# Products of ones in TensorE's idle stretches, and a last MLP product in two halves of the tokens, in an encoder layer on eight cores

## The chip, the cores and the metric

One Trainium2 chip, all eight cores, each with two of the sixteen sequences. The metric is device time in microseconds (us) of the slowest core. Some executions fell into a second, slower state: over 2300 us, with a lower granted TensorE clock on the cores of one die.

## The reference

One layer on x (16 x 2048 x 1024, float32): a grouped-query attention branch and a pooling branch with gates, a cross attention into 256 memory tokens, then the MLP and a final norm. The change touches only the end:

```python
def rmsnorm(x, g):
    xf = x.astype(jnp.float32)
    y = xf * lax.rsqrt(jnp.mean(xf * xf, axis=-1, keepdims=True) + EPS)
    return (y * g.astype(jnp.float32)).astype(x.dtype)
# ... attention, pooling, gates, cross attention ...
        n3 = rmsnorm(h, g_ffn[l])
        h = h + jnp.square(jax.nn.relu(n3 @ w_ff1[l])) @ w_ff2[l]
    return rmsnorm(h, g_final)
```

## The kernel before

The kernel is written as a graph of operations. A scheduler in the program, with its own model of durations, gives each engine a fixed order before anything runs; semaphores keep the order right on the chip. The tokens go through in eight blocks of 512 (two sequences of four). While one block is in its projections and MLP, the attention of the next fills TensorE's gaps; the last block has no next one. The end of a block:

```python
def ff2_step(j):                       # output rows j*128 .. j*128+127, 512 tokens
    def f():
        w = [weight("FB", j), weight("FB", 8 + j)]
        h, H, r = c_["h"][j], c_["H"], c_["r"]
        b = V("f2", "D")               # a PSUM bank
        PE([mm(lambda: ap(b), wsl(w[k // 16], k % 16 * 128), lambda k=k: ap(H[k]), k == 0, k == 31,
               [wk(w[k // 16], k % 16 * 128), H[k]]) for k in range(32)], [b])
        t = V("f2r", "M1")
        D(lambda e: e.tensor_tensor(out=ap(t), in0=ap(b), in1=ap(r), op=ALU.mult), 512, [b, r], [t])
        TT(lambda e: e.tensor_tensor(out=ap(h), in0=ap(t), in1=ap(h), op=ALU.add), [t, h], [h])
        if j >= 1:
            stat_after(j - 1, "s4")    # square on ScalarE, sum over rows by a product with ones
        if j == 7:
            stat_after(7, "s4")
            final()
    return f

def final():
    r = rstd(c_["s4"], 1024.0)         # Ln, then Exp, on ScalarE
    for kc in range(8):
        h = c_["h"][kc]
        D(lambda e, h=h, kc=kc: e.scalar_tensor_tensor(out=ap(h), in0=ap(h), scalar=vec[:, ...], in1=ap(r), ...), 512, ...)
        store(outT[s, tb, kc], lambda h=h: ap(h), 262144, [h], ...)
# ...
order, span, busy = schedule(G, pools, 100000.0, 40000.0)
# ...
emit(nc, st, order)
```

The softmax here doesn't subtract the row's maximum and nothing guards it: scores larger than these inputs give would overflow.

Of the kernel before, what the change touches and what calls it, by code (L numbers as in the profile page):

```python
# [13 lines left out]
EPS = 1e-6  # L14
# [59 lines left out]
NORM1 = (1, 4)  # L74
LAST_NORM = 1
SUMMED = ()
LATE = {("KV", i): 1 for i in range(3)}
LATE.update({("G", i): 1 + i % 2 for i in range(8)})
LATE.update({(name, i): i % 3 for i in range(16) for name in ("FA", "FB")})
# [326 lines left out]



def emit(nc, stack, order):
    engines = ("pe", "act", "dve", "pool", "sp")  # L410
    SEM_CAP = 20000
    allops = sorted((o for e in engines for o in order[e]), key=lambda o: o.place)
    dcount = {}
    plan = {}
    known = {e: {} for e in engines}
    clock = {}
    needed = set()

    def waits_for(e, deps):
        out = []  # L420
        kn = known[e]
        ds = sorted(deps, key=lambda d: -d.finish)
        for d in ds:
            if d.dma is not None:
                s, v = d.key
                if kn.get(("d", s), 0) >= v:
                    continue
                out.append(("d", s, v))
                kn[("d", s)] = v
            else:  # L430
                if d.eng == e and e == "pe":
                    continue
                if kn.get(d.eng, -1) >= d.order:
                    continue
                out.append(("e", d))
                needed.add(d)
                kn[d.eng] = d.order
            for k, v in clock[d].items():
                if kn.get(k, -1) < v:
                    kn[k] = v  # L440
        return out

    for o in allops:
        e = o.eng
        if o.mms is not None:
            pl = []
            pre = list(o.extra)
            for m in o.mms:
                ds = pre
                pre = []  # L450
                ds = ds + [d for d, off in o.deps.items() if m["at"] <= off < m["at"] + 1e-6]
                pl.append(waits_for(e, ds))
            plan[o] = pl
        else:
            plan[o] = waits_for(e, list(o.deps) + list(o.extra))
        if o.dma is not None:
            kn = known[e]
            idle = [s for s, c in dcount.items() if kn.get(("d", s), 0) >= 16 * c]
            s = min(idle, key=lambda s: dcount[s]) if idle else len(dcount)
            dcount[s] = dcount.get(s, 0) + 1  # L460
            o.key = (s, dcount[s] * 16)
            clock[o] = dict(known[e])
        else:
            c = dict(known[e])
            c[e] = o.order
            clock[o] = c
    cnt = {e: 0 for e in engines}
    ms = {}
    for e in engines:
        for o in order[e]:  # L470
            if o in needed:
                ms[o] = cnt[e]
                cnt[e] += 1
    esem = {e: [stack.enter_context(nc.semaphore(f"s_{e}{k}")) for k in range(max(1, -(-cnt[e] // SEM_CAP)))]
            for e in engines}
    dsem = {s: stack.enter_context(nc.semaphore(f"d_{s}")) for s in dcount}
    block = stack.enter_context(nc.Block())

    def do_waits(eng, ws):
        for w in ws:  # L480
            if w[0] == "d":
                eng.wait_ge(dsem[w[1]], w[2])
            else:
                k = ms[w[1]]
                eng.wait_ge(esem[w[1].eng][k // SEM_CAP], k % SEM_CAP + 1)

    def run(e, eng):
        for o in order[e]:
            if o.mms is not None:
                for m, ws in zip(o.mms, plan[o]):  # L490
                    do_waits(eng, ws)
                    ins = m["fn"](eng)
            else:
                do_waits(eng, plan[o])
                ins = o.fn(eng)
            if o.dma is not None:
                ins.then_inc(dsem[o.key[0]], 16)
            elif o in ms:
                ins.then_inc(esem[e][ms[o] // SEM_CAP], 1)

    @block.tensor
    def _(eng):
        run("pe", eng)

    @block.scalar
    def _(eng):
        run("act", eng)

    @block.vector
    def _(eng):  # L510
        run("dve", eng)

    @block.gpsimd
    def _(eng):
        run("pool", eng)

    @block.sync
    def _(eng):
        run("sp", eng)
        for s, c in dcount.items():  # L520
            eng.wait_ge(dsem[s], c * 16)
# [3 lines left out]
def build_core(info=None):  # L525
# [15 lines left out]
    with st:  # L541
# [16 lines left out]
        def V(name, pool):  # L558
            v = Val(name, pool)
            if pool == "D" and name not in ("ops", "sps", "s2", "s3", "s4"):  # L560
                v.alt = "E"
            return v
# [39 lines left out]
        def D(fn, n, R, W, rate=1.0, ptr=0, port=False):  # L602
            return G.op((("dve", dve_t(n, rate) + 50.0 * ptr),), fn, R, W, port=port)
# [13 lines left out]
        def PE(mms, W):  # L617
            return G.op((("pe", 0.0),), None, (), W, mms=mms)
# [24 lines left out]
            return o  # L643


        def constants():
            load(lambda: vec[:], vec_d, 32768, [CONST["vec"]])
            load(lambda: rope[:], rope_d, 98304, [CONST["rope"]])
            for i in range(2):
                b = V("bandraw", "M2")  # L650
                load(lambda b=b: ap(b)[:, 0:864], band_d[i], 442368, [b])
                copy_any(lambda i=i: band[:].rearrange("p a n -> p (a n)")[:, i * 864:(i + 1) * 864],
                         lambda b=b: ap(b)[:, 0:864], 864, [b], [(CONST["band"], i)], psum=False, rate=2.0)
            b = V("pwraw", "M2")
            load(lambda b=b: ap(b)[:, 0:512], poolw_d, 262144, [b])
            copy_any(lambda: poolw[:], lambda b=b: ap(b)[:, 0:512], 512, [b], [CONST["poolw"]], psum=False, rate=2.0)
            D(lambda e: e.memset(ones[:], 1.0), 128, [], [CONST["ones"]])
            D(lambda e: e.memset(bd[:], 0.0), 128, [], [CONST["bd"]])
            D(lambda e: e.memset(bd[0:64, 0:64], 1.0), 64, [], [CONST["bd"]])
            D(lambda e: e.memset(bd[64:128, 64:128], 1.0), 64, [], [CONST["bd"]])  # L660
            D(lambda e: e.tensor_scalar(out=nbg[:], in0=vec[:, C_BG:C_BG + 16], scalar1=-1.0, scalar2=None, op0=ALU.mult),
              16, [CONST["vec"]], [CONST["nbg"]])
# [457 lines left out]
        def chain_steps(s, tb, lead, nxt):  # L1120
# [144 lines left out]
            def ff2_step(j):  # L1265
# [3 lines that stand above are left out]
                    b = V("f2", "D")  # L1269
# [6 lines that stand above are left out]
                        stat_after(j - 1, "s4")  # L1276
                    if j == 7:
                        stat_after(7, "s4")
                        final()
                return f  # L1280

            def final():
                r = rstd(c_["s4"], 1024.0)
                for kc in range(8):
                    h = c_["h"][kc]
                    D(lambda e, h=h, kc=kc: e.scalar_tensor_tensor(out=ap(h), in0=ap(h),  # L1286
                                                                   scalar=vec[:, C_GFINAL + kc:C_GFINAL + kc + 1], in1=ap(r),
                                                                   op0=ALU.mult, op1=ALU.mult), 512, [h, r, CONST["vec"]], [h], ptr=1, port=True)
                    store(outT[s, tb, kc], lambda h=h: ap(h), 262144, [h], [dram(("out", s, tb, kc))])
# [20 lines left out]
                part["xo"].append((16 * 216, gate_step(nxt[0], nxt[1], 1)))  # L1310
            part["f1"] = [(8 * 216, ff1_step(j)) for j in range(32)]
            part["f2"] = [(32 * 216 + 54, ff2_step(j)) for j in range(8)]
            return part


        blocks = [(s, tb) for s in range(2) for tb in range(4)]
# [58 lines left out]
        order, span, busy = schedule(G, pools, 100000.0, 40000.0)  # L1375
        if info is not None:
            info.update(marks=marks, order=order, span=span, busy=busy, G=G)
        emit(nc, st, order)
    return nc

# [132 lines left out]
```

## Time and profile before

| | us |
|---|---|
| time, median of the first 3 runs | 2248.9 |
| spans of the cores in the profile | 2229.4 to 2251.2 |
| TensorE busy on the slowest core | 2138.2 (95%) |
| end of the last product to the end of the span | 13.9 |

What a spell, a stretch in which the granted clock is 0.5, looks like in the work: These are TensorE rows of the slowest core in order of time (start us, duration us, engine, line, operation, out<-in, shapes, count, and in brackets the idle time before with its releaser):

```profile
2105.22 0.38 PE L613 MATMUL ps<-S_p,ones_bf 128*128 128x512 bf16 x1 [0.71 <-ACT S_p L1214]
2105.43 0.59 PE L613 MATMUL ps<-S_p,W_p 128*128 128x512 bf16 x2
...
2107.13 11.13 PE L613 MATMUL ps<-S_p,W_p 128*128 128x512 bf16 x33 [1.10 <-DVE S_p L1226]
```

33 products with 512 columns take 11.13 us, 337 ns each on the mean: those within the spell (2107.4 to 2114.2 us) start mostly 427 ns apart, and the later ones every 216 ns. No long gap stands before them, but idle stretches of 0.71 and 1.10 us, together half of the 3.4 us before the spell.

The traces show a pattern in this. On each core, all spells begin on one grid of 3.41 us. I read the stretches of these grids from 30 to 2200 us on 70 core records of twelve profiles. At full clock and with TensorE busy for under 42%, all 186 stretches were followed by a spell; between 42 and 64%, 130 of 868; above that, none of some 43000. That fits with the same gaps bringing a spell on one core and none on another, by where its grid lies (before, the gap of 2.3 us near 540 to 548 us is on cores 3, 4 and 5, and only core 5 has a spell there); and the rule of the change, which fills up to 70%, aims just above the highest share that a spell followed.

So the two things to tell apart are an idle stretch and the slow stretch that follows it: the first stays when something else is put into the gap, the second needn't (with the change, the clock lost up to 2200 us falls from 14.3 to 5.3 us).

### The profile page before, as it was taken

The numbers are of one execution on the slowest core, as the hardware profiler recorded it, in microseconds if no ns is written. First come the engines' busy times: TensorE is split into PE (matmuls) and PEld (weight loads), VectorE is DVE, ScalarE is ACT, GpSimd is POOL, SyncE is SP. The second block draws the span as 40 slices with busy tenths as digits, with TensorE's granted clock in tenths as the row PEclk, the third lists the DMA queues.
The fourth block names the chain that finished last, engine by engine and source line by source line (L and its number), as shares of the span: only waits on it lengthen the run. The fifth ranks groups of instructions, "written<-read, shape, count | busy, mean of one in ns | idle before, by whom it ended". The sixth has DMA issues, their size and how long they took to land.

```text
span 2251.2 us, 33586 instructions; the slowest of 8 cores (2229.4 to 2251.2 us)
## 1 busy us (share of the span) xinstructions
PE 2138.2 (95%) x10822; PEld 906.4 (40%) x10822; DVE 1469.2 (65%) x1754; ACT 1492.0 (66%) x1883; POOL 419.4 (19%) x304
## 2 busy tenths in 40 slices
PE   7978899989999999999999999999999999999997
PEld 3432333433434434444434444344434443444343
DVE  5877787669866687665874588557764677456402
ACT  6867788748885477853788368844786368835551
POOL 2332221124232231221110022002110121000100
PEclk9999999999999999999999999999999999999999
DMA  9976976999496882935633462435533463336342
GB/s 288 309 228 192 297 234 209 296 286 325 166 297 210 289 289 94 322 115 196 211 115 127 152 210 97 140 122 189 167 122 121 155 211 116 128 132 217 128 142 75
DMA packets 139707, 434.46 MB, mean 193 GB/s; under 512 B 15632, under 2 KB 15760, under 8 KB 139536
## 3 DMA queue, kind: packets, MB, share of 16 engines
q1 hardware_dynamic: 139536, 432.30, 58.8%
q8 instruction: 92, 1.51, 0.3%
q14 instruction: 79, 0.65, 0.1%
HBM read 368.28 MB, written 63.96 MB: 192 GB/s over the span
## 4 chain that ended last, share of the span: by engine, by line
PE 80%; DMA 7%; DVE 4%; ACT 3%; issue 3%; SPq 1%; POOL 0%; DVEq 0%; ACTq 0%; POOLq 0%
PE ps L613 80%; DMA M_p<-wst 4%; DMA wsc<-W_p 1%; ACT M_p L1031 1%; SPq L621 1%; DVE M_p L725 1%; DMA outT<-M_p 1%; DMA M_p<-xT 1%; ACT W_p L633 1%; DVE M_p L1286 1%; DMA M_p<-n1d 0%; DVE M_p L636 0%; ACT M_p L720 0%; DVE M_p L1042 0%; DVE M_p L1043 0%
## 5 line engine op out<-in xcount | busy, mean ns | idle before, releaser
L613 PE MATMUL ps<-S_p,W_p 128*128 128x512 bf16 (+1 forms) x6144 | 1370.6, 378 | 19.2 <-ACT W_p L633 5.7
L613 PEld LDWEIGHTS ps<-S_p,W_p 128*128 128x128 bf16 x6144 | 585.0, 98 | 772.2 <-issue 109.8
L1031 ACT ACTIVATE M_p<-ps 128x2048 bf16<-128x2048 f32 x256 | 479.5, 1873 | 226.3 <-PE ps L613 219.4
L1042 DVE TENSOR_TENSOR M_p<-M_p 128x1024 f32<-128x1024 f32 x224 | 285.2, 1273 | 180.6 <-ACT M_p L1031 173.7
L613 PE MATMUL ps<-M_p,W_p 128*128 128x512 bf16 x1600 | 380.6, 386 | 10.6 <-DVE M_p L725 5.6
L1043 DVE TENSOR_TENSOR M_p<-M_p 128x1024 f32<-128x1024 f32 x224 | 314.3, 1403 | 15.9
L709 POOL TENSOR_TENSOR M_p<-M_p 128x512 f32<-128x512 f32 x72 | 111.7, 1552 | 811.2 <-ACT M_p L700 778.2
L613 PEld LDWEIGHTS ps<-M_p,W_p 128*128 128x128 bf16 x1600 | 153.9, 99 | 218.2 <-issue 48.5
L700 ACT ACTIVATE M_p<-M_p 128x512 f32<-128x512 f32 x216 | 133.1, 624 | 114.3 <-DVE M_p L1238 44.2
L636 POOL CAST W_p<-M_p 128x1024 bf16<-128x1024 f32 x96 | 122.0, 1277 | 425.9 <-PE ps L613 232.3
L1257 ACT ACTIVATE M_p<-ps 128x512 f32<-128x512 f32 x256 | 151.9, 593 | 53.3 <-PE ps L613 51.2
L1273 DVE TENSOR_TENSOR M_p<-ps,M_p 128x512 f32<-128x512 f32 x64 | 44.3, 692 | 209.5 <-PE ps L613 209.4
L613 PE MATMUL ps<-S_p,KV_p 64*128 64x512 bf16 x1024 | 157.2, 385 | 16.9 <-ACT M_p L1031 12.9
L613 PE MATMUL ps<-M_p,KV_p 128*64 128x512 bf16 x1024 | 137.1, 389 | 22.2 <-ACT M_p L1031 17.9
L1261 ACT ACTIVATE S_p<-M_p 128x512 bf16<-128x512 f32 x219 | 137.9, 629 | 19.9 <-ACT M_p L1257 0.4
L633 ACT ACTIVATE W_p<-M_p 128x1024 bf16<-128x1024 f32 x71 | 74.1, 1054 | 113.0 <-PE ps L613 73.2
L1109 ACT ACTIVATE M_p<-ps,nbg 128x512 f32<-128x512 f32 x128 | 86.5, 684 | 54.0 <-PE ps L613 52.8
L613 PEld LDWEIGHTS ps<-M_p,KV_p 128*64 128x64 bf16 x1024 | 49.7, 109 | 99.9 <-issue 75.8
L636 DVE CAST W_p<-M_p 128x1024 bf16<-128x1024 f32 x57 | 42.7, 771 | 57.4 <-DMA M_p<-wst 22.8
L613 PEld LDWEIGHTS ps<-S_p,KV_p 64*128 64x128 bf16 x1024 | 29.8, 94 | 124.1 <-issue 124.0
L613 PE MATMUL ps<-S_p,ones_bf 128*128 128x512 bf16 x166 | 55.9, 395 | 22.9 <-ACT S_p L700 14.4
L613 PE MATMUL ps<-W_p,M_p 128*128 128x384 bf16 (+1 forms) x512 | 76.9, 305 | 0.0
(80 smaller groups left out, 1669.4 us busy)
## 6 DMA issues: line engine op xcount, KB each, us to landing
W_p<-wsc SPq DMA_DIRECT2D x383, 512.0 KB, 4.2
M_p<-wst SPq DMA_DIRECT2D x228, 512.0 KB, 9.0
wsc<-W_p SPq DMA_DIRECT2D x69, 512.0 KB, 8.8
M_p<-xT SPq DMA_DIRECT2D x128, 256.0 KB, 8.7
outT<-M_p SPq DMA_DIRECT2D x64, 256.0 KB, 5.5
n1d<-M_p SPq DMA_DIRECT2D x28, 256.0 KB, 8.0
M_p<-n1d SPq DMA_DIRECT2D x28, 256.0 KB, 6.1
pdd<-M_p SPq DMA_DIRECT2D x14, 256.0 KB, 8.7
```

The source lines that it names most:

```text
L613: return e.matmul(out(), lhsT=lhsT(), rhs=rhs(), start=start, stop=stop, skip_group_check=True, **kw)
L633: return e.activation(out=dst(), in_=src(), func=AF.Copy)
L636: return e.tensor_copy(out=dst(), in_=src())
L700: A(lambda e: e.activation(out=ap(sq), in_=src(), func=AF.Square), 512, False, R, [sq])
L709: TT(lambda e: e.tensor_tensor(out=ap(out), in0=ap(acc), in1=ap(sq), op=ALU.add), [acc, sq], [out])
L1031: A(lambda e: e.activation(out=b16(P).rearrange("p (a n) -> p a n", n=512), in_=ps[:, 0:4, :], func=AF.Exp, scale=0.125), 2048, True, S, [P])
L1042: D(lambda e: e.tensor_tensor(out=ap(acc), in0=ap(acc), in1=lo(), op=ALU.add), 1024, [P, acc], [acc], port=True)
L1043: D(lambda e: e.tensor_tensor(out=ap(acc), in0=ap(acc), in1=hi(), op=ALU.add), 1024, [P, acc], [acc], port=True)
L1109: A(lambda e, b=b, i=i: e.activation(out=ap(Et)[:, i * 512:(i + 1) * 512], in_=ap(b), func=AF.Exp, bias=nbg[:, i * 8 + j:i * 8 + j + 1], s ...
L1257: A(lambda e: e.activation(out=ap(rl), in_=ap(b), func=AF.Relu), 512, True, [b], [rl])
L1261: e.activation(out=ap(H), in_=ap(rl), func=AF.Square))
L1273: D(lambda e: e.tensor_tensor(out=ap(t), in0=ap(b), in1=ap(r), op=ALU.mult), 512, [b, r], [t])
```

## The change

The intent is twofold: hold TensorE's clock by giving it work in its idle stretches, and shorten the path after the last product. The diff, cut to its core:

```diff
+FILL = 216.0
+WARM_MIN, WARM_MARGIN, WARM_SPAN, WARM_SHARE = 500.0, 450.0, 3400.0, 0.7
+def keep_warm(G, order, make):
+    # ... gaps: TensorE idle over WARM_MIN in the schedule's own time ...
+    def bank(a, b):                     # a PSUM bank that is free over the whole gap
+        for key, h in sorted(hist.items()):
+            k = bisect_right([x[0] for x in h], a) - 1
+            if k >= 0 and h[k][1] + 200.0 <= a and (k + 1 == len(h) or h[k + 1][0] >= b):
+                return key, h[k][2].ops
+            if k < 0 and h[0][0] >= b:
+                return key, []
+        return None
+    for g in gaps:
+        room[g[0]] = int((g[2] - g[1] - WARM_MARGIN) / FILL)
+    for w in range(0, n - span, 4):     # windows of 3.4 us: fill until 70% busy, as far as the room goes
+        need = int(WARM_SHARE * span - busy[w:w + span].sum()) + 1
+        # ... g[3] += 1 while need > 0 and g[3] < room ...
+    at = {g[0]: g for g in gaps if g[3]}
+    # ... make(bank, count, the bank's last users) is put before the operation behind the gap ...

+            def ff2_half(hf, j):        # as ff2_step, for the tokens hf*256 .. hf*256+255
+                    kept = c_.setdefault("fb", {})
+                    w = kept.pop(j) if j in kept else [weight("FB", j), weight("FB", 8 + j)]
+                    if hf == 0 and j >= 4:
+                        kept[j] = w
+                    PE([mm(lambda: ap(b)[:, 0:256], wsl(...), lambda k=k: ap(H[k])[:, c0:c1], ..., n=256) for k in range(32)], [b])
+                    # ... the rest on 256 tokens; behind the eighth product final_half() ...
+            if nxt is None:
+                part["f2"] = [(16 * 216 + 54, ff2_half(0, j)) for j in range(8)] + [(16 * 216 + 54, ff2_half(1, j)) for j in range(7, -1, -1)]

+        def filler(bank, n, before):
+            # ...
+            o.mms = [mm(lambda: ps[:, k, :].rearrange("p (a n) -> p a n", n=128), lambda: ones[:],
+                        lambda: ones[:].unsqueeze(1).to_broadcast([128, 4, 128]), True, True, []) for _ in range(n)]

+        filled = keep_warm(G, order, filler)
         emit(nc, st, order)
```

More of the change, by code (lines that the diff above doesn't have):

```diff
@@ L405, in schedule @@
     return order, span, busy
+def keep_warm(G, order, make):
+    hist = {}
+    for o in G.ops:
+        for v in o.allocs:
+            if v.pool in ("E", "D") and v.ops[0] is o:
+                hist.setdefault((v.pool, v.slot), []).append((o.start, max(x.finish for x in v.ops), v))
+    for h in hist.values():
+        h.sort(key=lambda x: x[0])
+    pe = order["pe"]
+    gaps = []
+    end = 0.0
+    for i, o in enumerate(pe):
+        if o.start - end > WARM_MIN:
+            gaps.append([i, end, o.start, 0])
+        end = o.start + o.dur
+    step = 50.0
+    n = int(end / step) + 1
+    busy = np.zeros(n + 1)
+    for o in pe:
+        a, b = int(o.start / step), int((o.start + o.dur) / step)
+        busy[a:b + 1] = 1.0
+    span = int(WARM_SPAN / step)
+    cell = FILL / step
+    def bank(a, b):
[6 more added lines that the diff above has]
+        return None
+    room = {}
+    for g in gaps:
+        room[g[0]] = int((g[2] - g[1] - WARM_MARGIN) / FILL)
+    starts = [g[1] for g in gaps]
+    for w in range(0, n - span, 4):
+        need = int(WARM_SHARE * span - busy[w:w + span].sum()) + 1
+        if need <= 0:
+            continue
+        a, b = w * step, (w + span) * step
+        for g in gaps[max(bisect_left(starts, a) - 1, 0):bisect_right(starts, b)]:
+            while need > 0 and g[3] < room[g[0]]:
+                x = int(g[1] / step + g[3] * cell)
+                if x + cell > w + span:
+                    break
+                g[3] += 1
+                before = busy[w:w + span].sum()
+                busy[x:x + int(cell) + 1] = 1.0
+                need -= busy[w:w + span].sum() - before
+    new = []
+    at = {g[0]: g for g in gaps if g[3]}
+    n_fill = 0
+    for i, o in enumerate(pe):
+        if i in at:
+            g = at[i]
+            found = bank(g[1], g[2])
+            if found is not None:
+                f = make(found[0], g[3], found[1])
+                f.eng, f.start, f.finish = "pe", g[1], g[1] + g[3] * FILL + PE_TAIL
+                f.place = o.place - 0.5
+                new.append(f)
+                n_fill += g[3]
+        new.append(o)
+    for k, o in enumerate(new):
+        o.order = k
+    order["pe"] = new
+    return n_fill
@@ L643, in copy_any @@
             return o
+        READY = []
         def constants():
@@ L656, in constants @@
             copy_any(lambda: poolw[:], lambda b=b: ap(b)[:, 0:512], 512, [b], [CONST["poolw"]], psum=False, rate=2.0)
-            D(lambda e: e.memset(ones[:], 1.0), 128, [], [CONST["ones"]])
+            READY.append(D(lambda e: e.memset(ones[:], 1.0), 128, [], [CONST["ones"]]))
             D(lambda e: e.memset(bd[:], 0.0), 128, [], [CONST["bd"]])
@@ L1280, in ff2_step, with f, stat, final_half @@
                 return f
+            def ff2_half(hf, j):
+                c0, c1 = hf * 256, hf * 256 + 256
+                def f():
+                    h, H, r = c_["h"][j], c_["H"], c_["r"]
+                    first = 0 if hf == 0 else 7
+                    if hf == 0:
+                        G.lw[(h, 1)], G.rd[(h, 1)] = list(G.lw[(h, 0)]), list(G.rd.get((h, 0), ()))
+                    kept = c_.setdefault("fb", {})
+                    w = kept.pop(j) if j in kept else [weight("FB", j), weight("FB", 8 + j)]
+                    if hf == 0 and j >= 4:
+                        kept[j] = w
+                    b = V("f2", "D")
+                    PE([mm(lambda: ap(b)[:, 0:256], wsl(w[k // 16], k % 16 * 128), lambda k=k: ap(H[k])[:, c0:c1], k == 0, k == 31,
+                           [wk(w[k // 16], k % 16 * 128), H[k]], n=256) for k in range(32)], [b])
+                    t = V("f2r", "M1")
+                    D(lambda e: e.tensor_tensor(out=ap(t)[:, 0:256], in0=ap(b)[:, 0:256], in1=ap(r)[:, c0:c1], op=ALU.mult), 256,
+                      [b, r], [t])
+                    D(lambda e: e.tensor_tensor(out=ap(h)[:, c0:c1], in0=ap(t)[:, 0:256], in1=ap(h)[:, c0:c1], op=ALU.add), 256,
+                      [t, (h, hf)], [(h, hf)], port=True)
+                    sq = V("sq", "S1")
+                    A(lambda e: e.activation(out=ap(sq)[:, 0:256], in_=ap(h)[:, c0:c1], func=AF.Square), 256, False, [(h, hf)], [sq])
+                    c_.setdefault("sqs", []).append(sq)
+                    if j != first:
+                        stat(j)
+                    if j == 7 - first:
+                        stat(j)
+                        final_half()
+                def stat(j):
+                    i = c_["ns"] = c_.get("ns", -1) + 1
+                    if i % 8 == 0:
+                        c_["s4"] = V("s4", "D")
+                    b, sq = c_["s4"], c_["sqs"].pop(0)
+                    PE([mm(lambda: ap(b)[:, 0:256], lambda: ones[:], lambda: ap(sq)[:, 0:256], i % 8 == 0, i % 8 == 7,
+                           [CONST["ones"], sq], n=256)], [b])
+                def final_half():
+                    b = c_["s4"]
+                    r = V("rstd", "M1")
+                    A(lambda e: e.activation(out=ap(r)[:, 0:256], in_=ap(b)[:, 0:256], func=AF.Ln, bias=EPS, scale=1.0 / 1024.0),
+                      256, True, [b], [r])
+                    A(lambda e: e.activation(out=ap(r)[:, 0:256], in_=ap(r)[:, 0:256], func=AF.Exp, scale=-0.5), 256, False, [r], [r])
+                    for kc in range(8):
+                        h = c_["h"][kc]
+                        R = [(h, hf), r, CONST["vec"]]
+                        def fn(e, h=h, kc=kc):
+                            return e.scalar_tensor_tensor(out=ap(h)[:, c0:c1], in0=ap(h)[:, c0:c1],
+                                                          scalar=vec[:, C_GFINAL + kc:C_GFINAL + kc + 1], in1=ap(r)[:, 0:256],
+                                                          op0=ALU.mult, op1=ALU.mult)
+                        D(fn, 256, R, [(h, hf)], ptr=1, port=True)
+                        store(outT[s, tb, kc][:, c0:c1], lambda h=h: ap(h)[:, c0:c1], 131072, [(h, hf)],
+                              [dram(("out", s, tb, kc, hf))])
+                return f
@@ L1312, in chain_steps @@
             part["f2"] = [(32 * 216 + 54, ff2_step(j)) for j in range(8)]
-            return part
+            if nxt is None:
+                part["f2"] = [(16 * 216 + 54, ff2_half(0, j)) for j in range(8)] + [(16 * 216 + 54, ff2_half(1, j)) for j in range(7, -1, -1)]
+            return part
+        def filler(bank, n, before):
+            o = Op()
+            o.engs, o.fn, o.dma, o.deps, o.extra, o.vals, o.allocs = (("pe", 0.0),), None, None, {}, list(before), [], []
+            o.vals = []
+            k = bank[1] + (4 if bank[0] == "D" else 0)
+            o.mms = [mm(lambda: ps[:, k, :].rearrange("p (a n) -> p a n", n=128), lambda: ones[:],
+                        lambda: ones[:].unsqueeze(1).to_broadcast([128, 4, 128]), True, True, []) for _ in range(n)]
+            for i, m in enumerate(o.mms):
+                m["at"] = i * FILL
+            o.deps = {x: 0.0 for x in READY}
+            o.dur = n * FILL
+            return o
         blocks = [(s, tb) for s in range(2) for tb in range(4)]
@@ L1377, in build_core @@
             info.update(marks=marks, order=order, span=span, busy=busy, G=G)
+        filled = keep_warm(G, order, filler)
+        if info is not None:
+            info.update(filled=filled)
         emit(nc, st, order)
```

## The prediction

> **What bounds the kernel now.** I read the page first, then the cores, then the chain of waits, then the busy time by stretch around each place where the granted clock falls, then the last 60 us in order of time. From the page (slowest core; busy time and share of the span, and the chain that ended last by engine):
>
> ```profile
> span 2251.2 us, 33586 instructions; the slowest of 8 cores (2229.4 to 2251.2 us)
> ...
> PE 2138.2 (95%) x10822; PEld 906.4 (40%) x10822; DVE 1469.2 (65%) x1754; ACT 1492.0 (66%) x1883; POOL 419.4 (19%) x304
> ...
> PE 80%; DMA 7%; DVE 4%; ACT 3%; issue 3%; SPq 1%; POOL 0%; DVEq 0%; ACTq 0%; POOLq 0%
> ```
>
> TensorE is the bound: busy 95%, and 80% of the chain. Only about 113 us of the span (2251.2 - 2138.2) are idle. What can be won is idle time, or time in which TensorE is busy at half speed. The cores differ:
>
> ```profile
> core 1: 2242.5 us, clock 0.993
> core 2: 2245.9 us, clock 0.991
> core 3: 2233.3 us, clock 0.994
> ...
> core 5: 2251.2 us, clock 0.989
> ...
> core 7: 2251.0 us, clock 0.988
> ```
>
> The longest cores have the lowest clock. Core 5 lost 0.011 x 2251 = 25 us of clock; the stretch 2225 to 2252, where nothing is left to multiply for most of it, has 27 x (1 - 0.79) = 5.7 us of them. Some 19 us remain. Where they lie, with the columns stretch, its length, busy us (and count) of PE, PEld, DVE, ACT, POOL, granted clock, DMA share, GB/s:
>
> ```profile
> 35.00:45.00 10.00, 6.70 (x17) 2.25 (x18) 6.83 (x10) 6.36 (x12) 2.08 (x2) 0.69 1.01 317
> 97.00:107.00 10.00, 8.03 (x38) 2.65 (x37) 9.83 (x12) 7.21 (x7) 5.94 (x4) 0.83 1.03 343
> 165.00:185.00 20.00, 14.05 (x58) 4.21 (x56) 7.94 (x7) 14.51 (x13) 7.61 (x6) 0.74 0.84 266
> 223.00:231.00 8.00, 5.60 (x24) 1.28 (x21) 5.03 (x7) 5.16 (x7) 2.25 (x2) 0.79 0.97 328
> 543.00:552.00 9.00, 6.27 (x26) 1.78 (x26) 9.00 (x11) 7.29 (x7) 4.48 (x3) 0.81 1.01 311
> 669.00:679.00 10.00, 7.13 (x27) 2.35 (x26) 7.62 (x10) 6.50 (x9) 3.03 (x2) 0.83 1.00 376
> 799.00:809.00 10.00, 7.81 (x30) 3.04 (x28) 6.30 (x11) 5.58 (x10) 4.24 (x4) 0.83 1.06 311
> 2100.00:2118.00 18.00, 15.85 (x57) 5.93 (x56) 10.61 (x18) 7.03 (x13) 1.73 (x2) 0.81 0.19 58
> ```
>
> The reader is to see eight short spells and no general throttle. Between 860 and 2100 us the clock is 1.00 everywhere.
>
> The end of the run, from the chain of waits (start us, us, what):
>
> ```profile
> 2237.57 0.70 DVE M_p L1273
> ...
> 2238.37 0.70 DVE M_p L1274
> ...
> 2239.16 0.64 ACT S_p L700
> ...
> 2243.24 3.98 DVE M_p L1286 x6
> ```
>
> After the last product come two VectorE instructions, a square, a sum by ones, Ln, Exp, and eight gain products with eight stores: 2237.57 to about 2247.2. From there to the end 4.0 us pass (last store landing, final waits).
>
> [...] the spell in 543:552 costs 9 x 0.19 = 1.7 us of clock, a half of 3.4 us, and so do 669:679 and 799:809.[...] the spell near 2107 us follows an idle gap of 1.10 us with smaller ones before it.[...] a row of 12 such products takes 1.48 us and one of 4 takes 0.60 us, so eight more take 0.88 us, 110 ns each, weight loads hidden. For 512 columns, 32 take 7.07 us and 8 take 1.89 us: 216 ns.
>
> **The change, part by part.** *Filling.* Where the kernel's own schedule has TensorE idle over 0.5 us, products of ones (512 columns) into a free PSUM bank are put until windows of 3.4 us are 70% busy, leaving 0.45 us of each gap. Nothing is removed. They cost nothing if the gap is there on the chip, 216 ns each (427 cold) if not. Applied by hand to the gaps of four cores' traces, this rule gives 257 to 296 products, estimated 270, or 58 us of TensorE work; half of them would lie before 270 us. TensorE busy should go from 2138 to about 2190 us.
>
> The gain is bounded by the clock lost times TensorE's duty in the spell. Before 125 us: 3.1 x 0.67 + 1.7 x 0.80 = 3.4 us, but DMA share is 0.97 to 1.03 there and the chain consists of load issues and of waits for x and weights: I count 0. In 165:185: 20 x 0.26 x 0.70 = 3.7 us, and the chain there, from 166.4 us on, is TensorE and ScalarE's exponentials in turn, with no DMA: counted in full. In 223:231: 1.7 x 0.70 = 1.2 us, under a wait of 6.99 us for a DMA in the chain: 0. In 543:552: 1.7 x 0.70 = 1.2 us, a gap that cores 3 and 4 show at the same instruction too (so the schedule surely has it), but with DMA share 1.01: half, 0.6. In 669:679 and 799:809: 2.5 us together, seen on core 5 and core 7 and not on core 3 or 4, so it comes from slow DMAs and no filling will be placed for it: 0. In 2100:2118: 3.4 x 0.88 = 3.0 us, nothing beside it: in full. Together 7.3 us.
>
> Against it: filling that doesn't fit. If 3% of the 58 us lie where TensorE isn't idle on the chip, that is 1.7 us; the 3% are my choice, low because the gaps of cores 3, 4 and 5 agree within 0.1 us in nearly all later places and each fill stops 0.45 us short.
>
> *The last block's second product in halves.* 256 products of 512 columns become 512 of 256: 512 x 109 - 256 x 216 = +0.5 us. Eight weight tiles of 512 KB are kept and eight loaded again (4 MB over some 28 us, 150 GB/s, where DMA is at 12 to 44%): hidden. The first half's norm and stores lie behind the second half's products. On the path after the last product, VectorE and ScalarE instructions shrink by 256 columns each.[...] Two VectorE (0.53), three ScalarE (0.64), one product of ones (0.11), eight gains (2.13): 3.4 us. The last eight stores have rows of 1 KB instead of 2 KB; the final 5 us ran at 380 GB/s, and I take 0.2 us back for smaller rows. Net 3.4 - 0.5 - 0.2 = 2.7 us.
>
> Sum: 2248.9 - 7.3 + 1.7 - 2.7 = 2240.6 us.
>
> **The rivals.** *A, the filling gets in the way.* The schedule is a model; where its gap isn't on the chip, each product delays TensorE, which is the bound. If 20% misfit: +11.6 us in place of 1.7, about 2250. For it: the first 250 us are DMA-bound, and there order and gaps depend on loads. Against: TensorE waits there anyway. *B, cold spells are the cause of most of the spread between cores.* Core 3 is 18 us shorter than core 5 at 0.005 more clock (11 us), and most of the distance arises before 860 us. If spells also lengthen the later waits for loads and exponentials, the slowest core gains 14 to 16 us and the time is about 2230. Against: the stall that starts the spell can be what costs, and the fill leaves it. *C, nothing from filling.* The real spells follow late DMAs that the schedule doesn't know, and the waits that remain take up the saved time: only the tail is left, about 2246. *D, the tail is bound by its stores*: eight issues and 1 MB with small rows end no earlier; the tail then gives 1 us in place of 2.7.
>
> **Range and chances.** The parts move it by a few us each: 2229 (B with some misfit) to 2249 (A, or C with D) should hold it 8 times in 10. Faster by over 2% needs under 2204 us; core 3 without any spell and with the shorter tail would be at 2233.3 - 8 - 2.7 = 2223 (0.006 x 2233 = 13.4 us of clock, less 5.7 at the end), so 2%. Slower by over 2% needs 45 us, four fifths of all filling misplaced: 1%. Within 2%: 97%.
>
> **What would show it.** Right: mean clock of all cores at 0.994 or more, the spells in 165:185, 223:231 and 2100:2118 gone, those near 673 and 803 possibly left on some core; about 270 rows of ones times ones; TensorE busy near 2190; end of last product to end of span 10.5 us instead of 13.9; the spacing of the halved products 109 ns. Wrong: spells gone and the span unmoved (C), TensorE's progress between 270 and 2100 us slower than before (A), or cores equal near 2230 (B).

The forecast came to 2240.6 us. Cut is what it said of the hardware without showing it from this case. With that went its ground for giving the filling no cost in power, so the sum simply has no such term, and the rates per column from which the 3.4 us of the path after the last product were reckoned. The terms of those 3.4 us: the traces bear them out. In the trace before, casts out of PSUM take 0.29, 0.55 and 0.69 us for 128, 384 and 512 columns on VectorE and 0.27, 0.49 and 0.60 us on ScalarE; by an estimate from the first and the last of these, 256 columns less are 0.26 and 0.22 us less. In the trace after, it is 0.27 us on VectorE (0.69 to 0.42) and 0.21 us on ScalarE (0.63 to 0.42). The 0.2 us for the stores' smaller rows is the author's guess; what the rows did is under "The tail". "Such products" are those with 256 columns, and the 109 ns is what the trace before shows most often (108 to 110 ns) between the starts of two of them. The cold 427 ns are those of the rows above, and in the spell of 543:552 the clock is 0.50 for 3.41 us (547.46 to 550.87).

## More of the kernel before

Only executions in the fast state are compared. Verdicts give the ratio to the kernel before with a 95% interval.

## The result, and the profile after

The time is 2240.45 us (median of 4 runs, the slow one among them; 2239.56 to 2240.97 in the three fast ones, 2347.07 in the slow one) against 2248.82 us (4 runs). The ratio is 0.996, interval 0.994 to 0.998: within 2%. All ratios here are the mean time of one kernel's fast runs over that of the other's of the same rounds, so not quite the ratio of the medians that are quoted.

The page after (slowest core; busy, share, count; chain by engine):

```profile
span 2239.4 us, 34659 instructions; the slowest of 8 cores (2222.8 to 2239.4 us)
...
PE 2169.5 (97%) x11304; PEld 950.0 (42%) x11304; DVE 1474.8 (66%) x1778; ACT 1493.3 (67%) x1893; POOL 421.6 (19%) x304
...
PE 81%; DMA 7%; DVE 5%; ACT 3%; issue 3%; SPq 1%; POOL 0%; DVEq 0%; ACTq 0%; POOLq 0%
```

TensorE is busier and the span is shorter. The cores:

```profile
core 0: 2239.4 us, clock 0.996
core 1: 2225.0 us, clock 0.997
...
core 3: 2236.1 us, clock 0.997
...
core 7: 2222.8 us, clock 0.998
```

The clock is near full on all of them, and yet they still differ by 16.6 us (21.8 before). Core 1 has core 3's clock and is 11 us shorter. The same stretches as before, on the slowest core (the last one moved, as the program is shorter; columns as in the prediction):

```profile
97.00:107.00 10.00, 7.89 (x30) 2.56 (x30) 9.83 (x12) 6.08 (x7) 4.61 (x4) 0.66 1.03 327
165.00:185.00 20.00, 19.40 (x103) 7.53 (x100) 15.45 (x12) 18.25 (x17) 10.19 (x7) 1.00 0.79 266
223.00:231.00 8.00, 5.90 (x33) 1.82 (x34) 7.22 (x7) 7.06 (x8) 1.69 (x1) 1.00 1.01 338
543.00:552.00 9.00, 7.90 (x40) 2.78 (x39) 8.79 (x13) 6.14 (x8) 0.00 (x0) 1.00 1.00 321
669.00:679.00 10.00, 10.00 (x47) 3.74 (x43) 9.51 (x13) 7.94 (x10) 1.52 (x2) 0.83 0.66 235
2090.00:2108.00 18.00, 17.72 (x83) 7.87 (x82) 10.41 (x18) 8.66 (x16) 1.67 (x1) 1.00 0.27 88
```

The spells near 170, 227, 547 and 2105 us are gone on this core. The one near 100 us is there and longer, one near 670 us is there too, and one near 154 us is new. The filling by its tile, TensorE's row (count; duration ns min/median/max; first and last start us):

```profile
L688 PE MATMUL ps<-ones_bf x218: 377/379/631, 1.5 to 2230.2; 128*128 128x512 bf16 x109
```

218 products were put in, not 270. The end, from the chain of waits:

```profile
2229.82 0.43 DVE M_p L1376
...
2230.35 0.44 DVE M_p L1378
...
2230.87 0.42 ACT S_p L1381
...
2233.67 2.38 DVE M_p L1408 x6
```

From the first of these to the last gain product's end (2236.05) are 6.2 us, where it was 9.6 us before. From the end of the last MLP product to the end of the span it is 9.8 us; 10.5 was forecast, from 13.9. The halved products start 109 to 110 ns apart, as forecast.

Since the cores differ by loads that come early or late, I read one more thing from the traces: when the n-th real product starts (filling not counted, and counted from 0), on every core whose record is complete. The table holds means of six cores of one profile each, us. "Clock lost" is the sum of (1 - clock) x time up to 2200 us, mean of eight cores. "Tail" is from the start of the last product of the MLP to the end of the span. The names are explained with the runs; the change's third profile is left out, for a reason given there.

| kernel | 600th product | 4000th | 4000th to 10000th | 10000th to 10558th | from there to the last | tail | clock lost |
|---|---|---|---|---|---|---|---|
| before | 128.7 | 846.4 | 1198.5 | 128.2 | 56.1 | 14.1 | 14.3 |
| the change | 126.6 | 838.6 | 1199.2 | 127.2 | 57.2 | 9.9 | 5.3 |
| the change, again | 128.0 | 840.8 | 1198.5 | 127.1 | 57.2 | 9.9 | 5.5 |
| filling alone | 127.8 | 840.8 | 1198.8 | 127.1 | 56.1 | 14.1 | 4.9 |
| halves alone | 128.6 | 847.4 | 1198.5 | 128.5 | 57.2 | 9.9 | 18.6 |
| filling of 8 columns | 128.3 | 844.9 | 1199.3 | 128.0 | 57.2 | 9.9 | 16.0 |
| no early filling | 129.3 | 844.2 | 1198.7 | 127.1 | 57.2 | 9.9 | 9.6 |
| early filling trimmed | 127.8 | 844.1 | 1199.2 | 127.2 | 57.2 | 9.9 | 10.9 |
| no filling in the last block | 127.5 | 838.5 | 1199.1 | 128.6 | 57.2 | 9.9 | 7.9 |
| less in the last block | 128.9 | 840.9 | 1199.5 | 127.0 | 57.2 | 9.9 | 5.3 |
| overfilled late | 128.4 | 839.7 | 1211.5 | 136.4 | 57.2 | 9.9 | 5.1 |
| any bank | 127.2 | 838.3 | 1198.5 | 127.0 | 57.2 | 9.9 | 2.8 |

Without a spell, the last block's column repeats to 0.1 us from core to core, and so do the two to the right of it; the steady part (4000th to 10000th) varies by 1 to 5 us. Up to the 4000th, the cores of one profile differ by 10 to 18 us, so a difference of 2 us there means little.

### The profile page after: what moved, and what is told of

It reads as the page before. It is cut to its first block, busy times and chain, and to the rows that moved or that the text cites. A ratio compares the mean times of both kernels' runs of the same rounds, so it can differ in the third digit from the quotient of the medians.

```text
span 2239.4 us, 34659 instructions; the slowest of 8 cores (2222.8 to 2239.4 us)
## 1 busy us (share of the span) xinstructions
PE 2169.5 (97%) x11304; PEld 950.0 (42%) x11304; DVE 1474.8 (66%) x1778; ACT 1493.3 (67%) x1893; POOL 421.6 (19%) x304
## 4 chain that ended last, share of the span: by engine, by line
PE 81%; DMA 7%; DVE 5%; ACT 3%; issue 3%; SPq 1%; POOL 0%; DVEq 0%; ACTq 0%; POOLq 0%
PE ps L688 81%; DMA wsc<-W_p 3%; DMA M_p<-wst 2%; ACT M_p L1108 1%; DVE M_p L802 1%; DMA outT<-M_p 1%; DMA M_p<-xT 1%; SPq L696 1%; DVE M_p L1120 0%; DVE W_p L711 0%; ACT W_p L708 0%; DVE M_p L1420 0%; DMA M_p<-n1d 0%; DVE M_p L711 0%; DVE M_p L1119 0%
## 5 line engine op out<-in xcount | busy, mean ns | idle before, releaser
L688 PEld LDWEIGHTS ps<-S_p,W_p 128*128 128x128 bf16 x6400 | 610.2, 98 | 745.9 <-issue 106.2
L688 PE MATMUL ps<-M_p,W_p 128*128 128x512 bf16 x1600 | 372.5, 380 | 6.9 <-DVE M_p L802 3.1
L1350 DVE TENSOR_TENSOR M_p<-ps,M_p 128x512 f32<-128x512 f32 x56 | 38.7, 691 | 113.3 <-PE ps L688 113.3
L711 DVE CAST W_p<-M_p 128x1024 bf16<-128x1024 f32 x57 | 42.7, 771 | 57.9 <-DMA M_p<-wst 21.4
L1189 ACT ACTIVATE M_p<-M_p 128x1024 f32<-128x1024 f32 x64 | 67.6, 1056 | 4.3 <-ACT M_p L1186 0.4
```

Source lines behind the costliest of these rows:

```text
L688: return e.matmul(out(), lhsT=lhsT(), rhs=rhs(), start=start, stop=stop, skip_group_check=True, **kw)
L711: return e.tensor_copy(out=dst(), in_=src())
L1189: A(lambda e: e.activation(out=ap(Et), in_=ap(Et), func=AF.Ln, bias=1.0, scale=1.0), 1024, False, [(Et, 0), (Et, 1)], [(Et, 0), (Et, 1)])
```

## The experiments

Eleven runs were made, and all gave correct results. My theory, "clock": the filling wins by keeping TensorE at full clock, the halves win the tail, and the two add up. The rivals stand with each run.

### Filling alone

```diff
-            if nxt is None:
+            if False:
                 part["f2"] = [(16 * 216 + 54, ff2_half(0, j)) for j in range(8)] + [...]
```

> The filling alone, the last block's second product whole as before. Theory clock (the filling wins by keeping TensorE at full clock, the halves win the tail, and the two add up): 5 to 7 us under the kernel before, ratio 0.997; mean clock 0.995 or more on every core; from the last product to the end 14.1 us as before. Theory tail (nearly all of the measured 8 us is the shorter tail and the filling is neutral): ratio 1.000, no more than 2 us under the kernel before.

Ratio 0.9979 (0.9965 to 0.9994), 2248.0 against 2252.5 us. That is 4.7 us, a little under the expected 5 to 7, and clear of 1. The clocks are 0.994 to 0.998 (0.995 was expected on every core). The tail is 14.1 us. So there is a gain without the shorter tail, and the theory that the filling is neutral is out; that it gives more than the 2 us which that theory allowed isn't shown, as the interval reaches from 1.4 to 7.9 us.

### Halves alone

```diff
-        filled = keep_warm(G, order, filler)
+        filled = 0
```

> The halves alone, no filling. Theory clock: 3.1 us under the kernel before, ratio 0.9986; tail 9.9 us in place of 14.1, the 512 half products 1.1 us longer than the 256 whole ones; mean clock and cold spells as before (0.988 to 0.995). Theory tail: ratio 0.9965, as the whole change.

Ratio 0.9985 (0.9966 to 1.0005), 2250.0 us: 3.4 us, and the interval includes 1. The trace is firmer than the time: the tail is 9.9 us and the products take 57.2 us in place of 56.1, on every complete core. Clocks are 0.989 to 0.992 and the spells are those of before. The two parts' gains, 4.7 and 3.4 us, add up to 8.1; the whole gave 0.4% of 2248.8, 9.0 us. That agrees, but each of the three is known to about 4 us only.

### Filling with 8 columns

```diff
-            o.mms = [mm(lambda: ps[:, k, :].rearrange("p (a n) -> p a n", n=128), lambda: ones[:],
-                        lambda: ones[:].unsqueeze(1).to_broadcast([128, 4, 128]), True, True, []) for _ in range(n)]
+            o.mms = [mm(lambda: ps[:, k, 0:8], lambda: ones[:], lambda: ones[:, 0:8], True, True, []) for _ in range(n)]
```

> The whole change, but each filling product has 8 columns in place of 512: the same places, waits, banks and count, and next to no activity (218 x 25 to 60 ns instead of 47 us). Theory clock: the cold spells of before come back, mean clock 0.988 to 0.995, and the time is that of the halves alone, ratio to before 0.9986. Theory order (the filling wins by something else than activity, such as its waits changing when TensorE goes on): the gain of the whole change stays, ratio 0.9965.

The trace before has products of 8 columns too: they start mostly 25 to 29 ns apart, those of 512 columns 216 ns. The clock does what the theory says: 0.990 to 0.994, clock lost 16.0 us as without filling, and a last block of 128.0 us. The time is 0.9978 (0.9963 to 0.9994), 2246.8 us. This lies nearer to the halves alone (0.9985) than to the change (0.996), but the interval doesn't part it from either. So activity, not the added waits, holds the clock; that the whole gain in time hangs on it isn't shown by this run alone.

### No early filling

```diff
+    for g in gaps:
+        if g[1] < 100000.0:
+            g[3] = 0
     at = {g[0]: g for g in gaps if g[3]}
```

> The whole change without the 93 filling products of the first four places (the first 40 us, 43% of all filling, where on the chip they run over their gaps: the first key product starts at 20.7 us and not at 16.2). The prediction's step (nothing is won before 125 us, because loads set the pace there): the time of the whole change within 1.5 us, TensorE's 600th product at 125 to 129 us. Rival (the early clock matters, since the 600th product came 2.1 us earlier on the mean of the cores with the change): 2 us longer than the whole change, the 600th product back at 128 to 129 us.

Ratio 0.9966 (0.9949 to 0.9982), 2244.8 us, 0.06% from that of the change (in other rounds): 1.3 us, within the expected 1.5, but with intervals of nearly 4 us to each side the time doesn't exclude the rival's 2 us. The 600th product comes at 129.3 us on the mean (128.1 to 131.5), a little later than either theory had it; in the seven profiles of the table with all of the early filling it comes at 126.6 to 128.9. The 126.6 us of the change's first profile, which had made me doubt the prediction's zero, didn't come back: the change again gave 128.0 us.

### The change once more, and a third time

> The change as it is, once more, as the reference for the runs beside it on one chip. Ratio to before 0.996, as at first (0.994 to 0.998); mean clock 0.995 to 0.998.

Ratio 0.996 (0.9941 to 0.998), 2244.6 against 2252.9 us. As expected.

> The change as it is, a third time, as the reference for the next run on the same chip. Ratio to before 0.996; spells left near 100 and 138 us on most cores.

Ratio 0.9985 (0.9963 to 1.0007), 2248.2 against 2250.8 us: not as expected. Its fast runs scatter from 2237.8 to 2252.3 us, and the profiled one had a whole die at a clock of 0.81 for 156 to 159 us. Core 5 of that die, then core 1 of the other, same columns as before:

```profile
70.00:220.00 150.00, 143.96 (x758) 61.54 (x758) 110.83 (x129) 109.43 (x130) 49.15 (x39) 0.81 0.73 229
...
226.00:300.00 74.00, 65.45 (x326) 24.75 (x325) 60.70 (x78) 54.08 (x62) 20.73 (x18) 1.00 0.93 307
```

```profile
70.00:220.00 150.00, 130.17 (x790) 58.94 (x787) 119.13 (x137) 114.77 (x136) 54.21 (x40) 0.99 0.76 245
```

I take this for a short bout of the slow state, which the limit for it (a die over 1% longer) doesn't catch. In four of the five fast runs two or four cores of one die have means of 0.984 to 0.986; no other fast run with filling shows this, and none of the eight fast runs of the kernel before in these rounds has a core below 0.986, where such a bout would give about 0.976 (an estimate: 0.990 less 0.19 x 159 / 2250). Whether the filling brings such bouts on is open, and so it is for the slow state: slow executions (over 2300 us) were 12 of 53 with full-width filling, 4 of 37 of the kernel before and 2 of 12 of the other two. With these bouts, the gain of these rounds isn't clear of zero, and I rest nothing on this ratio, for or against.

### Less filling in the last block

```diff
+    for g in gaps:
+        if 2040000.0 < g[1] < 2200000.0:
+            g[3] = 7 if g[3] > 7 else 0
     at = {g[0]: g for g in gaps if g[3]}
```

> The change with less filling in the last block, where 24 products (5.2 us of work) stand and TensorE has no idle time left behind any of them: 7 of the 15 at the longest gap, none at the four others. Theory overrun (part of these 24 doesn't fit its gap and delays the real products): the stretch from the 10000th to the 10558th real product, 127.1 us with the change on every core, falls to about 126.5 us, since the fastest core of before took 127.9 us with one cold spell that cost it about 1.4 us. Rival (all 24 fit, and fewer let the clock fall): the stretch goes to 127.9 us or more and a spell of 3.4 us stands near 2100 us again.

The edit leaves one of the four other places (a single product just outside its limits), so 16 products are gone, not 17. Ratio 0.995 (0.993 to 0.9969), 2243.4 against 2244.6 us for the change in the same rounds: not told apart. The stretch is 127.0 us on all cores and no spell is there. Both expectations miss: taking away 3.5 us of filling wins 0.15 us, so nearly all of it had fitted (127.15 less 126.99 us on the mean), and 7 products hold the clock as well as 15 do.

### No filling in the last block

```diff
+    for g in gaps:
+        if 2040000.0 < g[1] < 2200000.0:
+            g[3] = 0
     at = {g[0]: g for g in gaps if g[3]}
```

> The change without the 24 filling products of the last block, all else as it is: what one spell costs. Theory clock: a spell of 3.4 or 6.8 us near 2100 us on nearly all cores, and the stretch from the 10000th to the 10558th real product at 127.9 to 129.1 us, as with the kernel before, in place of 127.1. Rival (the filling doesn't matter there): 127.0 us without a spell.

Again one product stays, so 23 are gone. One run, state unknown: 2247.65 us, not compared. Its trace is the clearest of all. The spell is back on seven of the eight cores; the six cores with complete records take 128.1 to 129.3 us for the stretch, where the change and the kernel with less filling take 127.0 to 127.2. Core 1 at this place, first without the filling, then (in the run with less) with 7 products:

```profile
2095.00:2115.00 20.00, 17.62 (x66) 6.75 (x64) 11.23 (x18) 8.54 (x15) 1.83 (x2) 0.83 0.20 67
```

```profile
2075.00:2095.00 20.00, 18.39 (x84) 7.79 (x82) 10.99 (x18) 10.86 (x19) 1.68 (x1) 1.00 0.33 106
```

Against the change's 127.15 us, a spell of 3.4 us costs 0.9 to 1.5 us here, one of 6.8 us 2.2 us. This is the mechanism: with one edit at one place the spell and its cost come back.

### Overfilled late

```diff
+    for g in gaps:
+        if g[3] and 1000000.0 < g[1] < 2200000.0:
+            g[3] += 10
     at = {g[0]: g for g in gaps if g[3]}
```

> The change with 10 more products at each of the 12 places with filling between 1000 us and the end of the last block's scores: 120 more, 26 us of TensorE work. It measures what a product costs that doesn't fit. By the traces, TensorE is still idle 0.35 to 0.68 us behind the filling at 6 of the 12 places, 3 us together; the rest overruns. Expected: 22 to 24 us longer than the change, or about 0.19 us for each added product; busy 97% to 98%. If filling were harmless (the engine had slack that these stretches hide): less than 5 us.

Ratio 1.005 (1.003 to 1.0071), 2265.9 us, 21.4 us over the change's median in the same rounds. In the trace, 70 more products cost 13.0 us between the 4000th and the 10000th, and 50 more cost 9.3 us in the last block: 0.19 us each on the mean, as expected. Filling is free only while it fits (in the run with less of it, 3.5 us of it had cost 0.15 us).

### Early filling trimmed

```diff
+    for g in gaps:
+        if g[1] < 100000.0:
+            g[3] = min(g[3], 24 if g[1] == 0.0 else 8)
     at = {g[0]: g for g in gaps if g[3]}
```

> The change with the first four places cut from 38, 30, 3 and 22 products to 24, 8, 3 and 8, so that they no longer run over their gaps: the first real product back from 12.0 to about 7 to 8.5 us, the first key product from 20.2 to about 17 us. Theory loads (the first 125 us are set by loads): the 600th product at 127 to 129 us and the time that of the change within 1.5 us. Rival (the overrun costs what it delays): 3 to 4 us shorter than the change.

The first filling does run over. In the change, slowest core, in order of time:

```profile
1.47 11.16 PE L688 MATMUL ps<-ones_bf 128*128 128x512 bf16 x38 [1.47 <-DVE bd_bf L735]
12.47 1.89 PE L688 MATMUL ps<-S_p,ones_bf 128*128 128x512 bf16 x8
14.19 6.64 PE L688 MATMUL ps<-ones_bf 128*128 128x512 bf16 x30
20.67 1.89 PE L688 MATMUL ps<-M_p,W_p 128*128 128x512 bf16 x8
```

The first key product waits behind 30 products of ones and starts at 20.7 us (20.2 on the mean of the cores). Trimmed, it starts at 17.0 us on the mean, but both kernels reach the 16th real product at 21.8 to 21.9 us, since the eight key products take about 4.8 us in the trimmed kernel (21.8 - 17.0) and 1.6 us in the change (21.8 - 20.2), and the trimmed one loses more clock (10.9 us in the table, against 5.3 and 5.5). Ratio 0.996 (0.9941 to 0.9978), 2245.3 us: the change's time within 0.7 us, and the means of the fast runs are equal (2244.9 us). So the overrun doesn't cost the rival's 3 to 4 us. One thing stays open: in this profile and in that without early filling, the mean core reaches the 4000th product at 844.1 and 844.2 us, and with all of it at 838.3 to 840.9. Much of it lies in one stretch: from the 800th to the 900th real product (about 165 to 190 us) the mean core takes 25.5 us in these two profiles and 23.4 us in six with all of the early filling, and spells between 160 and 186 us stand on 8 of 16 cores, in those six on 2 of 48. The filling of that stretch is the same in all of them. So the early filling may act on what comes later, a path that neither theory had; with no difference in the times, it isn't settled.

### Filling with any bank that comes free

```diff
     def bank(a, b):
+        best = None
         for key, h in sorted(hist.items()):
-            k = bisect_right([x[0] for x in h], a) - 1
-            if k >= 0 and h[k][1] + 200.0 <= a and (k + 1 == len(h) or h[k + 1][0] >= b):
-                return key, h[k][2].ops
-            ...
+            k = bisect_right([x[0] for x in h], b - 1.0) - 1
+            if k < 0:
+                return key, [], a
+            if (k + 1 == len(h) or h[k + 1][0] >= b) and h[k][0] < b:
+                t = max(a, h[k][1])
+                if best is None or t < best[2]:
+                    best = (key, h[k][2].ops, t)
+        return best
     # and: g[3] = min(g[3], int((g[2] - found[2] - WARM_MARGIN) / FILL)), and the cut in the last block
```

> The change with filling also where it found no PSUM bank: at gaps of 2.3 and 3.4 us (near 98 and 136 us on the chip), 1.4 and 1.6 us (near 214 and 280 us) the schedule has TensorE idle, but no bank is free 0.2 us before the gap begins, so the change puts nothing there. Here the bank that comes free first within the gap is taken: 7, 5, 3 and 3 products more; and the last block's filling is cut to 7 products as in the run with less of it. Theory banks (the spells near 100 and 138 us are left because filling found no bank): these two spells go on most cores, mean clock 0.998 or more. In time: each spell costs up to 1.7 us, on the path only where no load sets the pace; I expect 0 to 3 us under the change (ratio to before 0.995). Rival (they come from late loads, which no filling reaches): the spells stay.

The filling's own semaphore waits keep the bank's last readers safe. The spells near 100 and 138 us are gone on all eight cores. In the change's three profiles 18 of 24 cores have one near 100 us and 9 of 24 one near 138 us (28 of 56 with the other four profiles of the same early filling). So the theory of banks is right. Core 4 in the first of the two stretches, with this kernel and then with the change:

```profile
97.00:107.00 10.00, 9.00 (x47) 3.37 (x47) 9.83 (x10) 8.02 (x8) 5.57 (x4) 1.00 1.04 356
```

```profile
97.00:107.00 10.00, 7.85 (x28) 2.64 (x28) 9.83 (x12) 5.98 (x6) 3.08 (x3) 0.66 1.05 347
```

Two cores have no spell at all up to 2200 us, and the clock is 0.997 to 0.999 (0.998 or more was expected). The time is 0.9973 (0.9953 to 0.9994), with only three fast runs of six (2241.5 to 2245.2 us): no better than the change can be told. Why not? Its cores:

```profile
core 1: 2243.2 us, clock 0.997
...
core 3: 2223.3 us, clock 0.999
```

Twenty microseconds at nearly one clock. At the 1200th product core 1 is 5 us behind core 3, at the 2400th 16 us. The chain of waits from 257 to 527 us on core 1, then on core 3, as shares:

```profile
by line: PE ps L696 51.2%; DMA wsc<-W_p 28.9%; issue 3.8%; DMA M_p<-wst 2.4%; SPq L704 2.3%; ACT M_p L1116 2.1%; DVE W_p L719 1.8%; POOL W_p L719 1.7%; DVE M_p L1128 1.4%; DVE M_p L1127 1.1%; ACT W_p L716 0.8%; DVE S_p L794 0.5%; ACT M_p L8
```

```profile
by line: PE ps L696 83.2%; DMA wsc<-W_p 6.5%; issue 2.4%; ACT M_p L1116 2.1%; ACT W_p L716 1.2%; ACT M_p L1342 1.1%; POOL W_p L719 0.9%; DVE W_p L719 0.5%; DVE M_p L1323 0.5%; ACT M_p L805 0.4%; SPq L704 0.3%; DVE S_p L794 0.3%; ACT M_p L78
```

In this profile the slowest core is one whose transfers (the writing of rounded weights to their scratch) come late. The slowest core in the three fast runs of the change was a different one each time in the lists of spans: 0, 2 and 3. What decides which core it is, I didn't test.

So no version was found that beats the change beyond the intervals.

## Why the prediction was right, and where its terms were not

The time (2240.45 us against 2240.6; the three fast runs have a median of 2239.94) held, and so did the mechanism: work in the idle stretches holds the clock (14.3 us of clock lost before, 5.3 with the change), and the halves shorten the tail (14.1 to 9.9 us). The closeness is partly luck: its terms are off by more than its sum.

- **What bounds.** TensorE, as read. In the steady part (4000th to 10000th) nothing moved: 1198.5 and 1199.2 us.
- **The filling's net gain.** Predicted 7.3 - 1.7 = 5.6 us. Measured 4.7 us alone; 5.6 us as the whole (9.0) less the halves (3.4). Two terms in it were mis-sized against each other. The last block's spell was put at 3.0 us; taking the filling away there cost 1.4 us on the mean and 2.2 us for a spell of 6.8 us, as long as the prediction's; from the kernel before to the change the mean fell by 1.0 us (128.2 to 127.2). The misfit was put at 1.7 us; it is about 0.2 us in the last block (less filling there won 0.15 us), and none can be seen in the steady part. The largest term, 3.7 us near 165 to 185 us (its product, 20 x 0.26 x 0.70, is 3.6), was too large for the mean core: from the 800th to the 900th real product it takes 25.8 us on 12 cores without filling (the kernel before and the halves alone) and 23.4 us on 36 cores with it (the change twice, the filling alone, and the three runs that edit only later filling), 2.4 us less. Another gain stands in no term: from the 2200th to the 2400th product, near 475 to 520 us, the same cores take 46.8 and 45.2 us, 1.6 us less.
- **Zero before 125 us.** The times show no loss without the early filling beyond their noise, but they don't prove a zero, and the open point above speaks against it. That filling would run over was in the rival A, but not that it runs over in the load-bound start, where the overrun cost nothing that the times show.
- **The count.** 270 products were estimated and 218 came. The hand count used gaps on the chip; the schedule has some of them smaller (the gap of 3.77 us near 168 us got one product), and its rule needs a bank free over the whole gap, which the prediction overlooked. Banks account for at least 18 of the 52 missing, those that the run with any bank added. TensorE busy rose by 31 us, not by 52: 52 products fewer are 11 us of the difference; the rest should be real products that become shorter at full clock (216 ns apart in place of 427), which I hadn't counted.
- **Which spells go.** Right for those near 170, 547 and 2105 us, which no core of this profile has (near 170 us one core of the change's second profile has one), and for the one near 673 us, which one core kept. Near 229 us one core still had one. The spell near 100 us, to which the prediction gave no gain, stayed for want of a bank. Spells near 475 us (462 to 492 us), which the slowest core didn't have and no step named, were on 4 of 8 cores before (17 of 24 with the profiles of the halves alone and of 8 columns), and on none of 80 with full filling there.
- **The tail.** The path on the engines shrank from 9.6 to 6.2 us, the predicted 3.4: VectorE's two instructions went from 0.69 to 0.42 us and ScalarE's square from 0.63 to 0.42, as forecast. Casts don't all scale with the columns: in the trace before, ScalarE's take 0.60 us for 512 and 1.05 for 1024, VectorE's 0.69 and 0.77; on both, those of 512 read PSUM and those of 1024 SBUF. The stores were to cost 0.2 us more and in fact gave back about 0.7 us: from the last gain product's end to the end of the span it is 3.3 us (2239.4 - 2236.05), and was 4.0. In one stretch of 2 us each, the last stores moved 267 GB/s at a DMA share of 0.81 with rows of 1 KB, and 378 GB/s at a share of 1.00 with rows of 2 KB before: 13% less for the same busy share. The halves' products were to cost 0.5 us and cost 1.1; 0.9 of it can be worked out: 0.6 for the products at 109.2 ns, 0.2 for fourteen sums by ones at 0.109 us between them in place of six at 0.216, and 0.1 since the stretch ends at the start of a shorter product. The prediction had only the first. Net 3.1 us against 2.7.
- **Rivals.** A (misfit of 20%) is out, and the overfilled run shows what it would have cost. B (spells cause the spread of the cores, 2230 us) is out: with nearly all spells gone the cores still lie 16.6 and 19.9 us apart. C (nothing from filling) is out by the filling alone. D (stores bind the tail) is out.

## What to carry to other kernels

Where TensorE is the bound and its clock falls after short idle gaps, dummy products in those gaps win the slow stretch that follows, not the gap (here the clock lost fell from 14.3 to 5.3 us); those added beyond the room cost 0.19 us each here, so size them from gaps that are the same on every core and check that a free PSUM bank exists there. Splitting the last product along the tokens hides half of the final norm and its stores for the price of the extra instructions (here the tail went from 14.1 to 9.9 us and the products from 56.1 to 57.2); add up the path after the last product instruction by instruction: here that came out within 0.4 us net. When the metric is the slowest of eight cores, look at stretches of the trace on all cores: single terms of 1 us were clear there and lost in the times.
